# A WKV recurrence on one core: the first group's state steps moved ahead of later pairs, 65 fewer zero matmuls, and constants made later

## The chip, the core and the metric

The kernel runs on one core of a Trainium2 chip. The core has a matrix engine (PE, TensorE; its weight loads are listed as PEld), three engines for elementwise work (DVE, or VectorE; ACT, or ScalarE; POOL, or GpSimd) and SP, which here only issues DMAs. Every engine runs its own list of instructions in the order of the program, and waits on semaphores for the others. ACT and POOL issue DMAs too, each in the order of its own list. 16 DMA engines move the data between HBM and the on-chip memory SBUF; PE writes its results to PSUM, from where DVE and ACT read them.

The metric is the time of one launch in microseconds (us); lower is better.

## The reference

For 16 sequences of 2048 steps and 256 channels, a weighted sum with a decay `w` runs along the sequence, kept stable by a running maximum `pp`:

```
for t in range(seq_len):
    ww = u + kk                      # this step's own weight
    qq = np.maximum(pp, ww); e1 = np.exp(pp - qq); e2 = np.exp(ww - qq)
    output[b, t, :] = (e1 * aa + e2 * vv) / (e1 * bb + e2 + 1e-08)
    ww = pp - w + kk                 # state for the next step
    qq = np.maximum(ww, kk); e1 = np.exp(ww - qq); e2 = np.exp(kk - qq)
    aa = e1 * aa + e2 * vv; bb = e1 * bb + e2; pp = qq
```

Inputs are `k` and `v` (float32, 33.6 MB each), `w` and `u` (256 values each). The output has the shape of `v`.

## The kernel before, in words

**Tiling.** The sequence is cut into 16 groups of 128 steps, and each group into four "pairs" of 4 sequences: 64 pairs, n = 0 to 63, group c = n // 4. A pair is a tile of 128 time steps x 1024 (4 sequences x 256 channels), 0.524 MB of k and as much of v. Inside a pair the recurrence is a sum, done by PE with triangular matrices. Between groups a small state is carried.

**The steps of a pair**, with the names that the code gives them:

- LK, LV load k and v. RK rounds k for PE (DVE or POOL; pairs 3 to 10 do without, as their DMA rounds). CV casts v to bf16 (DVE for n < 10, then POOL).
- R q n and L q n (q = 0, 1): PE puts a row term and the triangular sum of k into one of two PSUM buffers X. X q n: ACT takes the exponential of it into EZR, which frees the buffer.
- TV: DVE multiplies by v. S: PE adds up the pair's totals into TOT.
- DEN, LN, INV: PE forms the denominator in an X buffer, ACT takes Ln and then Exp of the negative. NUM, MUL: PE forms the numerator, DVE multiplies. ST and SQ store the result; SQ is the last quarter of the store, from POOL, for some pairs near the end. They run some ten pairs behind the front (`LAG = 10`).

**The steps of a group**, after its fourth pair's S: CS (copy the totals), TU (PE turns them), SL (ACT, logarithms), FR and OF (DVE, frames and offsets), SW (ACT, weights), CH (DVE, the chain), SS (DVE, spread), TK (PE turns the result back), BK (DVE copies it to `cb`), and SN, KP, which hand the state to the next group. DEN and NUM of a group need its BK.

**The order** is written by a small planner at the end of the function. Each step has a place, a number near its pair's (tables `P`); steps are taken in order of place, as soon as what they come after has been issued and a buffer is free. `AT` overrides a place by name. The order that results is fixed in the program for each engine, which then only waits on semaphores.

**Zeros.** `zeros(m)` issues m matmuls of a zero tile into the PSUM tile TURN; they compute nothing that is used. 26 come at the start; then the planner puts `P["Z0"]` of them ahead of a step of pair 0 or group 0, and `P["Z"]` ahead of others. Between TK and BK, which use TURN, none is issued (`quiet`).

**Setup.** Before the planner runs, DVE clears WUf (a tile for the rows u and w), makes masks and constants, and sets the start values of the state tiles (U, G, TB, CB); POOL shapes the masks. `make_matrices` (step "mats", L182) and the start values (L230 to L236) stand on DVE ahead of the first RK.

In the profile L149 is a zero matmul, L201 R, L207 L, L210 X, L214 CV, L219 TV, L245 S, L251 CS, L258 TU, L262 SL, L267 and L269 FR, L273 to L275 OF, L281 SW, L285 and L288 CH, L295 SS, L302 TK, L306 BK, L322 DEN (into X) and NUM (into num), L330 LN, L338 INV, L350 MUL, L356 and L363 the stores, L194 RK, L108 and L111 LK, L115 LV, and L480 the end of the program.

Of the kernel before, what the change touches and what calls it, by code (L numbers as in the profile page):

```python
# [7 lines left out]
F32 = mybir.dt.float32  # L8
# [3 lines left out]
ACT = mybir.ActivationFunctionType  # L12
# [3 lines left out]
def kernel(  # L16
# [9 lines left out]
    K = tc.keep_in_program_order  # L26
    PE, DVE, SC, POOL, SP = nc.tensor, nc.vector, nc.scalar, nc.gpsimd, nc.sync
# [5 lines left out]
    D = 2 * Dm  # L33
    NP = 4 * NST
# [10 lines left out]
    RS = 2.0 ** -20  # L45
    CAP = 54.0
    BIG = 1e30
# [11 lines left out]
         "R": [-0.795, -7.965],  # L59
         "OUT": {"DEN": [-0.47, -0.155, -0.55, -0.495], "LN": [-11.935, -9.86, -0.84, -6.17], "INV": [-13.87, -8.32, -4.99, -5.82], "NUM": [-0.105, 0.155, 0.11, -5.15], "MUL": [1.115, 0.345, 0.895, 1.035], "ST": [-5.05, 7.26, 1.245, 7.765], "SQ": [-3.365, 6.69, -2.4, 8.84]},  # L60
         "TAIL": {"DEN": -4.36, "LN": -16.54, "INV": 3.8, "NUM": -0.31, "MUL": 4.39, "ST": 14.35, "step": 2.989, "SQ": 26.08},
         "Z0": {"L": 1, "S": 3, "DEN": 0, "NUM": 6, "TK": 47, "TU": 17, "R": 12},
         "Z": {"DEN": 0, "L": 1, "NUM": 0, "TK": 4, "S": 0, "TU": 1, "R": 0}}

    AT = {}

    consts = ctx.enter_context(tc.tile_pool(name="consts", bufs=1))
    kpool = ctx.enter_context(tc.tile_pool(name="kpool", bufs=NK))
# [3 lines left out]
    rpool = ctx.enter_context(tc.tile_pool(name="rpool", bufs=NRD))  # L72
# [14 lines left out]
    def matrix(name, dt):  # L87
        return consts.tile([128, 128], dt, tag=name, name=name)
# [10 lines left out]
    def how(n):  # L99
        return "D" if n < BYSP else FIRST[n] if n < len(FIRST) else PLAN[n % len(PLAN)]  # L100
# [4 lines left out]
    def load_k(n):  # L105
        if how(n) != "C":
            KR[n] = raw(opool, "ot") if n < BYSP else raw(kppool, "kf")
            K((SP if n < BYSP else POOL).dma_start(out=KR[n], in_=rows_of(k, n)))  # L108
        else:
            KR[n] = kpool.tile([128, 4, Dm], F32R, tag="kr", name="kr")  # L110
            K(POOL.dma_start(out=KR[n], in_=rows_of(k, n)))  # L111
# [6 lines left out]
    WUf = rpool.tile([128, 2, D], F32, tag="rd", name="WUf")[:, 0, 0:Dm]  # L118
# [2 lines left out]
    def row_wu(queue, x, g):  # L121
        K(queue.dma_start(out=WUf[g::32, :], in_=bass.AP(tensor=x.tensor, offset=x.offset, ap=[[0, 4], list(x.ap[0])])))

    K(DVE.memset(WUf, 0.0))
    load_k(0)
    row_wu(POOL, u, 1)
    row_wu(SC, w, 0)
# [50 lines left out]
    mats = {name: matrix(name, BF16) for name in ("Id", "IdN", "S", "SN")}  # L178
# [11 lines left out]
    X = [psx.tile([128, 2, D], F32, tag=f"X{a}", name=f"X{a}") for a in range(2)]  # L190
# [31 lines left out]
    AS, D1, L1, A0, FR, BC, A2 = range(7)  # L222
    U_of = [consts.tile([128, 7, 32, 3], F32, tag=f"U{j}", name=f"U{j}") for j in range(2)]
    G_of = [consts.tile([128, 3, 32, 3], F32, tag=f"G{j}", name=f"G{j}") for j in range(2)]
    TB_of = [consts.tile([128, 2, 32, 3], F32, tag=f"TB{j}", name=f"TB{j}") for j in range(2)]
    CB_of = [consts.tile([128, 4, 128], BF16, tag=f"CB{j}", name=f"CB{j}") for j in range(2)]
    AB = consts.tile([128, 2, 32, 3], F32, tag="AB", name="AB")
    st = {}

    for j in range(2):  # L230
        K(DVE.memset(CB_of[j].bitcast(F32), 0.0))
        K(DVE.memset(U_of[j][:, FR, :, 0:1], -BIG))
        K(DVE.memset(G_of[j][:, :, :, 0:1], 0.0))
    K(DVE.memset(U_of[0][:, D1, :, 0:1], -100.0))
    K(DVE.memset(U_of[0][:, L1, :, 0:1], 0.0))
    K(DVE.memset(TB_of[0][:, :, :, 0:1], 0.0))  # L236

    def sums(n):
        c, p = divmod(n, 4)
# [70 lines left out]
    RD, NUM, OT = {}, {}, {}  # L310
# [14 lines left out]
    def den(n, a):  # L325
        apply(X[a], n, ("S", "Id"), 1)

    def log_den(n, a):
        rd = rpool.tile([128, 2, D], F32, tag="rd", name="rd")
        K(SC.activation(rd, X[a], ACT.Ln, scale=RS))  # L330
        RD[n] = rd

    def parts(n):
        return (slice(0, 1), slice(1, 2)) if n == NP - 1 else (slice(0, 2),)

    def inverse(n):
        for i in parts(n):
            K(SC.activation(RD[n][:, i], RD[n][:, i], ACT.Exp, scale=-1.0))  # L338

    def by_x(n):  # L340
        return n >= NP - XT and n % 2 == 1
# [11 lines left out]
    def piece(n, h, queue):  # L353
        c, p = divmod(n, 4)
        t0 = c * TC + HS * (1 - h)
        K(queue.dma_start(out=out[4 * p + 2:4 * p + 4, t0:t0 + HS, :].rearrange("n t d -> t n d"), in_=OT[n][HS * h:HS * h + HS, 2:4, :]))  # L356

    def shared(n):
        return n >= BYPOOL or BYQ[n % len(BYQ)] == "P" and n >= BYF
# [5 lines left out]
            piece(n, h, SP)  # L365

    def store_rest(n):
        piece(n, 1, POOL)


    ops, free = {}, {"K": NK, "KP": NKP, "V": NV, "N": 1, "RD": NRD, "OT": NOT, "VB": NVB}
# [1 line left out]
    def step(name, place, fn, args=(), after=(), take=None, give=(), mode=0):  # L373
        key = name if isinstance(name, str) else " ".join(map(str, name))
        ops[name] = dict(place=AT.get(key, place), fn=fn, args=args, after=list(after), take=take, give=give, mode=mode)

    for n in range(NP):
        c, j = divmod(n, 4)
        early = n < BYSP
        vb = "OT" if n < VOT else "V"  # L380
        put = lambda key: n + P[key][j]
        lead = SOON * max(0.0, 1 - n / UNTIL)
        lag = LAG - sum(n < x for x in LAGS)
        m = n + lag - lead
        tail = n >= NP - LAG
        place = lambda key: m + (P["TAIL"][key] + (n - NP + LAG) * P["TAIL"]["step"] if tail else P["OUT"][key][int(n + lag + 2) % 4])
        kb = "OT" if early else "KP" if how(n) != "C" else "K"
        if n:
            step(("LK", n), n + P["LK"], load_k, (n,), [("LK", n - 1)], kb)
        else:  # L390
            free["OT"] -= 1
        step(("LV", n), n + P["LV"], load_v, (n,), [("LV", n - 1)] + ([("LK", n)] if n else []), vb)
        if how(n) != "C":
            step(("RK", n), put("RK"), round_k, (n,), [("LK", n), ("RK", n - 1)], "K", [kb])
        for q in range(2):
            step(("R", q, n), n + P["R"][q], rows, (n, q), ["wu", ("R", 1 - q, n - 1 + q)], "X", mode=3)
            step(("L", q, n), n + P["L"][q], logs, (n, q), [("R", q, n), ("LK", n), ("RK", n), ("L", 1 - q, n - 1 + q)], None,
                 ["K"] if q else [], 1)
            step(("X", q, n), n + P["X"][q], exps, (n, q), [("L", q, n), ("NUM", n - RING), ("S", n - RING)], None, ["X"])
        step(("CV", n), put("CV"), cast_v, (n,), [("LV", n), ("CV", n - 1)], "VB", [vb])  # L400
        step(("TV", n), put("TV"), times_v, (n,), [("X", 1, n), ("CV", n), ("TV", n - 1)], None, ["VB"])
        step(("S", n), put("S"), sums, (n,), [("TV", n), ("S", n - 1)] + ([("CS", c - 1)] if j == 0 else []), mode=2)
        if j == 3:
            s = P["STATE"][0 if c == 0 else 2 if c == NST - 1 else 1]
            for i, (name, fn, *after) in enumerate((
                    ("CS", copy_sums, ("S", n)), ("TU", turn, ("CS", c), ("CH", c - 1)), ("SL", state_logs, ("TU", c)),
                    ("FR", state_frames, ("SL", c), ("SN", c - 1)), ("OF", state_offsets, ("FR", c)),
                    ("SW", state_weights, ("OF", c)), ("CH", state_chain, ("SW", c), ("KP", c - 1)),
                    ("SS", state_spread, ("CH", c)), ("TK", turn_back, ("SS", c), "mats"), ("BK", copy_back, ("TK", c)),
                    ("SN", state_next, ("OF", c)), ("KP", state_keep, ("CH", c)))):  # L410
                if not (name in ("SN", "KP") and c + 1 == NST):
                    step((name, c), n + s[i] - lead * SHARE, fn, (c,), after, mode=1)
        step(("DEN", n), place("DEN"), den, (n,), [("BK", c), ("DEN", n - 1), "mats"], "X", mode=3)
        step(("LN", n), place("LN"), log_den, (n,), [("DEN", n), ("INV", n - 1)], "RD", ["X"])
        step(("INV", n), place("INV"), inverse, (n,), [("LN", n)])
        step(("NUM", n), place("NUM"), num, (n,), [("BK", c), ("TV", n), ("NUM", n - 1), "mats"], "X" if by_x(n) else "N", mode=3)
        step(("MUL", n), place("MUL"), mult, (n,), [("NUM", n), ("INV", n), ("MUL", n - 1)], "OT", ["X" if by_x(n) else "N", "RD"])
        step(("ST", n), place("ST"), store, (n,), [("MUL", n), ("ST", n - 1)], None, [] if shared(n) else ["OT"])
        if shared(n):
            step(("SQ", n), place("SQ"), store_rest, (n,), [("ST", n)], None, ["OT"])  # L420
    step("mats", P["mats"], make_matrices)
    step("wu", P["wu"], make_rows)

    quiet = False
# [60 lines left out]
```

## Time and profile before

| | us |
|---|---|
| median of 3 runs (lowest to highest) | 292.04 (290.93 to 292.12) |
| the profiled execution | 291.05 |
| its span, first to last instruction | 289.3 |
| busy in the span: PE, ACT, DVE, POOL | 272.0, 258.1, 246.1, 176.9 |

The mean clock granted to PE over the span is 0.988 of full speed. HBM is read for 67.12 MB and written for 33.55 MB.

How to read it. The page shows one execution: the busy time of each engine, the span in 40 slices of 7.2 us (a digit is the busy share in tenths, GB/s is what DMA moved), and groups of instructions. A row of the timeline has the start, the length in us, engine, line, operation, out<-in, shapes and count, and in brackets how long the engine had been idle before and who ended that. A row of sums by stretch has the stretch, its length, then busy time and instruction count of each engine, the granted clock, the DMA share and GB/s. A row of waits has who waited for whom, total us, times, longest. A row of one line's instructions has the count and the shortest, median and longest length in ns, then the first and last start. A `q` behind an engine's name is its sequencer, which issues DMAs and waits. A busy PE is not a PE at its peak, since matmuls are pipelined and their ends are modelled.

### The profile page before, as it was taken

The numbers are of one execution on the slowest core, as the hardware profiler recorded it, in microseconds if no ns is written. First come the engines' busy times: TensorE is split into PE (matmuls) and PEld (weight loads), VectorE is DVE, ScalarE is ACT, GpSimd is POOL, SyncE is SP. The second block draws the span as 40 slices with busy tenths as digits, with TensorE's granted clock in tenths as the row PEclk, the third lists the DMA queues.
The fourth block names the chain that finished last, engine by engine and source line by source line (L and its number), as shares of the span: only waits on it lengthen the run. The fifth ranks groups of instructions, "written<-read, shape, count | busy, mean of one in ns | idle before, by whom it ended". The sixth has DMA issues, their size and how long they took to land.

```text
span 289.3 us, 8057 instructions
## 1 busy us (share of the span) xinstructions
PE 272.0 (94%) x3263; PEld 139.5 (48%) x3263; DVE 246.1 (85%) x423; ACT 258.1 (89%) x290; POOL 176.9 (61%) x219
## 2 busy tenths in 40 slices
PE   7899999999999999999999999999999999997750
PEld 6445744444545455444545454554545455444330
DVE  6666889989898989899897979899898989797860
ACT  1587399999999999999999999999999999997890
POOL 7267367675767686675757686775757674422230
PEclk9999999999999999999999999999999999999995
DMA  7999999999999999999999999999999999896895
GB/s 229 351 347 347 348 343 337 382 328 392 386 393 380 371 387 377 393 383 392 391 381 382 385 385 388 392 365 397 391 391 382 389 363 390 294 247 180 221 265 147
DMA packets 58574, 101.21 MB, mean 350 GB/s; under 512 B 5152, under 2 KB 43560, under 8 KB 58536
## 3 DMA queue, kind: packets, MB, share of 16 engines
q0 software_dynamic: 21248, 65.55, 65.2%
q1 hardware_dynamic: 37280, 35.14, 36.3%
q8 instruction: 25, 0.41, 0.6%
q14 instruction: 13, 0.11, 0.1%
q10 hardware_dynamic: 8, 0.00, 0.0%
HBM read 67.12 MB, written 33.55 MB: 348 GB/s over the span
## 4 chain that ended last, share of the span: by engine, by line
PE 83%; DVE 4%; ACT 4%; issue 3%; POOL 1%; DMA 1%; POOLq 0%; SPq 0%; DVEq 0%
PE X L207 21%; PE X L322 15%; PE num L322 13%; PE X L201 12%; PE TURN L149 12%; PE TOT L245 7%; ACT EZR L210 2%; PE TOT L258 2%; DVE ot L350 1%; PE TURN L302 1%; POOL out_dram L356 1%; DMA out_dram<-ot 1%; ACT rd L330 1%; DVE EZR L219 1%; ACT rd L338 1%
## 5 line engine op out<-in xcount | busy, mean ns | idle before, releaser
L210 ACT ACTIVATE EZR<-X 128x1024 bf16<-128x1024 f32 x128 | 126.8, 1013 | 14.2 <-PE X L207 14.1
L214 POOL CAST vb<-vr 128x1024 bf16<-128x1024 f32 x54 | 56.3, 1042 | 69.7 <-DVE EZR L219 68.1
L219 DVE TENSOR_TENSOR EZR<-EZR,vb 128x2048 bf16<-128x2048 bf16 x64 | 77.8, 1218 | 0.4 <-ACT EZR L210 0.2
L350 DVE TENSOR_TENSOR ot<-num,rd 128x1024 f32<-128x1024 f32 x60 | 73.2, 1220 | 4.6 <-ACT rd L338 3.2
L338 ACT ACTIVATE rd<-rd 128x1024 f32<-128x1024 f32 (+1 forms) x65 | 67.9, 1046 | 2.0
L330 ACT ACTIVATE rd<-X 128x1024 f32<-128x1024 f32 x64 | 65.6, 1025 | 2.5 <-PE X L322 0.9
L149 PE MATMUL TURN<-Z 128*128 128x192 bf16 x319 | 55.7, 261 | 1.6 <-DVE Z L133 1.6
L201 PE MATMUL X<-WU,CO 64*64 64x512 bf16 x512 | 51.9, 390 | 1.1 <-DVE WU L176 0.9
L149 PEld LDWEIGHTS <-Z 128*128 128x128 bf16 x319 | 28.9, 101 | 48.9 <-issue 47.1
L115 POOL DMA_DIRECT2D vr<-in_v_dram x61 | 46.0, 753 | 6.5 <-DVE vb L214 6.5
L207 PE MATMUL X<-kr,NLE 128*128 128x512 f32 x128 | 45.6, 438 | 0.0
L207 PE MATMUL X<-kr,NLZ 128*128 128x512 f32 x128 | 45.5, 437 | 0.0
L108 POOL DMA_DIRECT2D kf<-in_k_dram x53 | 40.2, 758 | 0.0
L194 DVE CAST kr<-kf 128x1024 fp32r<-128x1024 f32 x39 | 30.6, 813 | 4.4 <-DMA kf<-in_k_dram 4.2
L201 PEld LDWEIGHTS <-CO 64*64 64x64 bf16 x512 | 15.7, 105 | 31.4 <-issue 26.4
L322 PE MATMUL X<-EZR,S 64*64 64x512 bf16 x256 | 26.2, 394 | 1.7 <-ACT rd L330 1.0
L322 PE MATMUL X<-cb,Id 64*64 64x512 bf16 x256 | 25.8, 376 | 0.0
L322 PE MATMUL X<-EZR,Id 64*64 64x512 bf16 x256 | 25.8, 376 | 0.0
L322 PE MATMUL num<-EZR,SN 64*64 64x512 bf16 x240 | 24.3, 386 | 1.1 <-DVE ot L350 1.1
L322 PE MATMUL num<-cb,IdN 64*64 64x512 bf16 x240 | 24.0, 376 | 0.0
L322 PE MATMUL num<-EZR,IdN 64*64 64x512 bf16 x240 | 23.9, 376 | 0.0
L245 PE MATMUL TOT<-EZR,OH 128*32 128x256 bf16 x512 | 23.4, 277 | 0.5 <-DVE EZR L219 0.5
(69 smaller groups left out, 270.0 us busy)
## 6 DMA issues: line engine op xcount, KB each, us to landing
vr<-in_v_dram POOLq DMA_DIRECT2D x61, 512.0 KB, 7.9
kf<-in_k_dram POOLq DMA_DIRECT2D x53, 512.0 KB, 8.8
out_dram<-ot SPq DMA_DIRECT2D x64, 256.0 KB, 10.2
out_dram<-ot SPq DMA_DIRECT2D x116, 128.0 KB, 10.1
kr<-in_k_dram POOLq DMA_DIRECT2D x8, 512.0 KB, 8.2
ot<-in_k_dram SPq DMA_DIRECT2D x3, 512.0 KB, 5.0
ot<-in_v_dram SPq DMA_DIRECT2D x3, 512.0 KB, 8.3
out_dram<-ot POOLq DMA_DIRECT2D x12, 128.0 KB, 3.3
```

The source lines that it names most:

```text
L115: K((SP if n < BYSP else POOL).dma_start(out=vr, in_=rows_of(v, n)))
L149: K(PE.matmul(TURN[:, 0:192], Z[:, 0:128], Z, start=first, stop=True, skip_group_check=True))
L201: K(PE.matmul(X[a][o:o + HS, i, :].rearrange("p (n d) -> p n d", n=2), CO[r:r + HS, q, :], WU[r:r + HS, :].unsqueeze(1).broadcast_to([HS, ...
L207: K(PE.matmul(X[a][:, i, :], (NLE, NLZ)[q], km[:, i, :], start=False, stop=True, skip_group_check=True))
L210: K(SC.activation(ez(n)[:, q, 1], X[a], ACT.Exp))
L214: K((DVE if n < EARLY else POOL).tensor_copy(vb, VR.pop(n)))
L219: K(DVE.tensor_mul(ez(n)[:, :, 0], ez(n)[:, :, 1], vb.unsqueeze(1).broadcast_to([128, 2, 2, D])))
L245: K(PE.matmul(t[32 * j:32 * j + 32, 0:256], OH[:, s:s + 32], ez(n)[:, 0, 1 - q, i, 256 * x:256 * x + 256], start=p == 0 and x == 0, stop=p ...
L322: K(PE.matmul(out_tile[o:o + HS, i, :], left, right, start=s == 0, stop=s == 2, tile_position=(r, o), skip_group_check=True))
L330: K(SC.activation(rd, X[a], ACT.Ln, scale=RS))
L338: K(SC.activation(RD[n][:, i], RD[n][:, i], ACT.Exp, scale=-1.0))
L350: K(DVE.tensor_mul(o.rearrange("p (i n) d -> p i (n d)", i=2)[:, i], NUM[n][:, i], RD[n][:, i]))
```

## The change

- **Zeros of pair 0 and group 0**: ahead of each R of pair 0 six instead of 12, ahead of TU 0 none instead of 17, ahead of TK 0 four instead of 47.
- **Places**: `AT` names some twenty steps. TU 0 to SW 0, TV 5, CV 6 and S 4 now stand ahead of pair 7's R; TV 6, CH 0 and SS 0 ahead of pair 8's; S 5, the four zeros, TK 0, BK 0 and S 6 between the two exponentials of pair 8; KP 0 moves behind pair 9, and CV 9 ahead of TV 8. BK 0 stood behind SL 1 before.
- **Quiet stretch**: with TK 0 and BK 0 next to each other, the single zeros ahead of L of pairs 8, 9 and 10 and of TU 1 are issued, seven in all. On PE 65 zeros fewer remain.
- **Constants**: `mats` and the start values (now a step "zero", `start_states`) come behind CV 1 on DVE instead of ahead of RK 0. WUf is cleared by POOL instead of DVE.
- **The last pair**: LN 63 is split in halves like INV 63, each half's Exp behind its Ln; its last quarter's store is issued by ACT instead of POOL.

The order of loads on SP and on POOL is the same in both, as is the order of all steps from RK 11 on, but for the last pair.

```diff
-         "Z0": {"L": 1, "S": 3, "DEN": 0, "NUM": 6, "TK": 47, "TU": 17, "R": 12},
+         "Z0": {"L": 1, "S": 3, "DEN": 0, "NUM": 6, "TK": 4, "TU": 0, "R": 6},
-    AT = {}
+    AT = {"TU 0": 5.01, "FR 0": 5.02, "SW 0": 6.2, "TK 0": 7.205, "CV 7": 6.4, "TV 5": 5.1, "S 4": 5.3, "S 5": 7.195, "TV 6": 6.3, "S 6": 7.21, "S 7": 8.1, "CH 0": 6.32, "SS 0": 6.33, "BK 0": 7.21, "CV 6": 5.2, "TV 7": 7.3, "KP 0": 8.6, "TV 8": 8, "R 0 6": 5.0, "R 0 8": 7.19, "R 0 9": 7.9}
...
-    K(DVE.memset(WUf, 0.0))
+    K(POOL.memset(WUf, 0.0))
...
-    for j in range(2):
-        K(DVE.memset(CB_of[j].bitcast(F32), 0.0))
...
+    def start_states():
+        for j in range(2):
+            K(DVE.memset(CB_of[j].bitcast(F32), 0.0))
...
+    def log_den(n, a):
+        RD[n] = rpool.tile([128, 2, D], F32, tag="rd", name="rd")
+        for i in parts(n):
+            K(SC.activation(RD[n][:, i], X[a][:, i], ACT.Ln, scale=RS))
+            if i.stop == 1:
+                invert(n, i)
+
+    def invert(n, i):
+        K(SC.activation(RD[n][:, i], RD[n][:, i], ACT.Exp, scale=-1.0))
+
     def inverse(n):
-        for i in parts(n):
-            K(SC.activation(RD[n][:, i], RD[n][:, i], ACT.Exp, scale=-1.0))
+        invert(n, parts(n)[-1])
...
-        piece(n, 1, POOL)
+        piece(n, 1, POOL if n < NP - 1 else SC)
...
-... ("SL", state_logs, ("TU", c)),
+... ("SL", state_logs, ("TU", c), "zero"),
...
-    step("mats", P["mats"], make_matrices)
+    step("mats", 1.0, make_matrices)
+    step("zero", 1.01, start_states)
```

More of the change, by code (lines that the diff above doesn't have):

```diff
@@ L228 @@
     st = {}
-    for j in range(2):
[L231 to L236, printed above, removed]
+    def start_states():
+        for j in range(2):
+            K(DVE.memset(CB_of[j].bitcast(F32), 0.0))
+            K(DVE.memset(U_of[j][:, FR, :, 0:1], -BIG))
+            K(DVE.memset(G_of[j][:, :, :, 0:1], 0.0))
+        K(DVE.memset(U_of[0][:, D1, :, 0:1], -100.0))
+        K(DVE.memset(U_of[0][:, L1, :, 0:1], 0.0))
+        K(DVE.memset(TB_of[0][:, :, :, 0:1], 0.0))
     def sums(n):
@@ L326, in den @@
         apply(X[a], n, ("S", "Id"), 1)
[L328 to L331, printed above, removed]
     def parts(n):
         return (slice(0, 1), slice(1, 2)) if n == NP - 1 else (slice(0, 2),)
+    def log_den(n, a):
[6 more added lines that the diff above has]
+        K(SC.activation(RD[n][:, i], RD[n][:, i], ACT.Exp, scale=-1.0))
     def inverse(n):
-        for i in parts(n):
-            K(SC.activation(RD[n][:, i], RD[n][:, i], ACT.Exp, scale=-1.0))
+        invert(n, parts(n)[-1])
     def by_x(n):
@@ L405 @@
             for i, (name, fn, *after) in enumerate((
-                    ("CS", copy_sums, ("S", n)), ("TU", turn, ("CS", c), ("CH", c - 1)), ("SL", state_logs, ("TU", c)),
+                    ("CS", copy_sums, ("S", n)), ("TU", turn, ("CS", c), ("CH", c - 1)), ("SL", state_logs, ("TU", c), "zero"),
                     ("FR", state_frames, ("SL", c), ("SN", c - 1)), ("OF", state_offsets, ("FR", c)),
```

## The prediction

> **What bounds the kernel now.** I read the page first, for who is busy; then sums by stretch, for how the start differs from the middle; then the timeline from 16 to 50 us, where every moved step lies; last the timeline of the end.
>
> ```profile
> PE 272.0 (94%) x3263; PEld 139.5 (48%) x3263; DVE 246.1 (85%) x423; ACT 258.1 (89%) x290; POOL 176.9 (61%) x219
> ACT  1587399999999999999999999999999999997890
> GB/s 229 351 347 347 348 343 337 382 328 392 386 393 380 371 387 377 393 383 392 391 381 382 385 385 388 392 365 397 391 391 382 389 363 390 294 247 180 221 265 147
> 3.00:40.00 37.00, 35.85 (x329) 21.60 (x328) 26.34 (x60) 22.08 (x24) 19.72 (x32) 1.00 1.28 350
> 50.00:250.00 200.00, 199.67 (x2444) 98.15 (x2437) 184.42 (x295) 196.82 (x223) 137.30 (x156) 1.00 1.04 383
> ```
>
> In the two sums the columns are length, busy time of PE, PEld, DVE, ACT and POOL, granted clock, DMA share, GB/s. From 50 to 250 us ACT has work for 196.82 of 200 us; that stretch is ACT's. In the fill, 3 to 40 us, ACT works 22.08 of 37, and PE's 35.85 contain the zero matmuls. The ACT row's "3" is the hole that the change aims at:
>
> ```profile
> 28.98 4.05 PE L149 MATMUL TURN<-Z 128*128 128x192 bf16 x47
> 34.84 2.02 ACT L210 ACTIVATE EZR<-X 128x1024 bf16<-128x1024 f32 x2 [4.38 <-PE X L207]
> ```
>
> ACT idles 4.38 us while PE does 47 zeros, the turn back (TK 0) and two sums ahead of pair 8. That is what one would like to win. But the DMA rate in the fill is flat (350 GB/s over the stretch, 343 to 351 in the second to sixth slice of 7.2 us), hole or no hole, and the consumers of loads tell when loads arrive:
>
> ```profile
> 16.98 0.73 DVE L214 CAST vb<-vr 128x1024 bf16<-128x1024 f32 x1 [0.79 <-DMA vr<-in_v_dram]
> 27.37 0.69 DVE L214 CAST vb<-vr 128x1024 bf16<-128x1024 f32 x1 [1.06 <-DMA vr<-in_v_dram]
> 39.40 1.04 POOL L214 CAST vb<-vr 128x1024 bf16<-128x1024 f32 x1 [1.62 <-DMA vr<-in_v_dram]
> 40.39 1.04 POOL L194 CAST kr<-kf 128x1024 fp32r<-128x1024 f32 x1
> 40.80 1.16 DVE L194 CAST kr<-kf 128x1024 fp32r<-128x1024 f32 x1 [1.16 <-DMA kf<-in_k_dram]
> ```
>
> These are CV 3, CV 6 and CV 10 waiting for v3, v6 and v10, then RK 11 without a wait, and RK 12 waiting for k12. From v6 to v10 are four pairs in 12.03 us, 3.01 us a pair. Two loads of 0.524 MB in 3.01 us are 348 GB/s, the whole rate of the windows. So loads come one each 1.50 us whatever the engines do, and k12, one load behind v10, is met 1.40 after it. The change keeps the order of all loads on SP and POOL, and nothing that it moves lets them start sooner. **These arrivals stay.**
>
> **The change, part by part.**
>
> *Zeros.* Ahead of R 0 0 and R 1 0 six go each, 17 ahead of TU 0, 43 ahead of TK 0: 72 out. TK 0 and BK 0 are now close together, so seven single zeros that lay in the quiet stretch between them come back (two for each of pairs 8, 9, 10, one ahead of TU 1). Net 65; at 4.05/47 = 0.086 us, 5.6 us of PE. What this reaches is decided by the arrivals.
>
> *Head.* WUf's memset goes from DVE to POOL, and the constants and start states (4.59 to 6.22) leave DVE ahead of RK 0.
>
> ```profile
> 0.93 0.27 DVE L124 MEMSET WUf<- 128x256 f32 x1 [0.93 <-PEq L469]
> 1.50 0.75 POOL L122 DMA_DIRECT2D WUf<-in_u_dram  x1 [0.99 <-DVE I L131]
> 4.59 0.27 DVE L231 MEMSET CB<- 128x256 f32 x1
> 6.22 0.68 DVE L194 CAST kr<-ot 128x1024 fp32r<-128x1024 f32 x1
> 7.87 0.41 PE L201 MATMUL X<-WU,CO 64*64 64x512 bf16 x4 [0.88 <-DVE WU L176]
> ```
>
> POOL idles 0.99 ahead of u's DMA, so a memset (about 0.26 at the 1.04 for 1024 elements of its cast above) fits in. The first R gains between 0 (the row u lands no sooner) and 1.6 us (6.22 less 4.59); the six zeros gone ahead of R 1 0 add 0.5. I take 1.0 in all for pairs 0 to 5, and it reaches nothing, as pair 6 meets its arrival. The 1.6 us of constants and states now stand ahead of CV 2 on DVE, which, its own work being 1.0 earlier, makes CV 2 about 0.6 late: hidden by DVE's wait for v3 up to 16.98. Without that cover 0.6 us would sit in front of S 1.
>
> *First group's steps.* TU 0, SL 0, FR 0, OF 0, SW 0 move ahead of pair 7, TK 0 and BK 0 behind pair 8, and TV 5, CV 6, S 4 to S 6 between. PE loses the hole, and then runs into the loads, which are issued k(n+1), v(n): v10 is at 39.3, so k11 at 37.8, v9 at 36.3, k10 at 34.8, and L 0 10 starts at 34.9 at best. On DVE the new order is CV 9 (v9, 36.3), TV 8, CS 1: 36.4 + 0.69 + 1.22 + 0.42 = 38.7. TU 1 then starts at about 38.75.
>
> ```profile
> 40.31 0.58 PE L258 MATMUL TOT<-Sel,ts 128*128 128x96 f32 x4
> 40.82 0.41 PE L322 MATMUL X<-EZR,S 64*64 64x512 bf16 x4
> 41.89 0.21 DVE L267 TENSOR_TENSOR U<-U 128x64 f32<-128x64 f32 x1
> 43.15 1.22 DVE L219 TENSOR_TENSOR EZR<-EZR,vb 128x2048 bf16<-128x2048 bf16 x1
> 43.22 0.71 PE L207 MATMUL X<-kr,NLE 128*128 128x512 f32 x2
> 44.88 0.62 PE L245 MATMUL TOT<-EZR,OH 128*32 128x256 bf16 x16
> 45.43 0.41 PE L322 MATMUL X<-EZR,S 64*64 64x512 bf16 x4
> 46.32 1.02 ACT L330 ACTIVATE rd<-X 128x1024 f32<-128x1024 f32 x1 [0.16 <-PE X L322]
> 49.40 0.41 PE L322 MATMUL X<-EZR,S 64*64 64x512 bf16 x4
> 50.28 1.03 ACT L330 ACTIVATE rd<-X 128x1024 f32<-128x1024 f32 x1
> ```
>
> From TU 1 (40.31) to L 0 11 (43.22) are 2.91 us of PE work: L 0 11 at 41.65, by when RK 11 (40.39 + 1.04 on POOL) is just done. R, L of pair 11 and S 8 take 44.88 - 43.22 = 1.66: PE is at S 9 at 43.3. S 9 needs TV 9, and TV 9 follows RK 12, which starts at 40.80 with k12 in both kernels; from 40.80 to 43.15 DVE is busy without a break, so TV 9 still ends at 44.37. S 9 at 44.4, DEN 1 at 44.77: **0.66 earlier than 45.43**. LN 1 follows (46.32, ACT then runs on). DEN 2 needs X(0,12) done and TK 1 out of the way: 48.85 for 49.40, LN 2 0.55 earlier. Of 5.6 us of zeros and a hole of 4.38, 0.55 is left on ACT.
>
> Does it stay through 200 us? ACT is 98.4% busy there, which speaks for it. Against it: DMA is at 383 GB/s, and DVE still meets loads:
>
> ```profile
> DVE kr L194 <- DMA kf<-in_k_dram: 3.1, 7, 0.6
> ```
>
> Seven times in 200 us (3.1 in all) RK waits for its k, and an earlier ACT only waits there longer, as at 40.80. Bounds: 0 and 0.66. I take 0.4, nearer to ACT's row, since DVE has 15.6 us of slack in that stretch to swallow such waits.
>
> *End.* The last pair's Ln is split in halves, and the last quarter's store (SQ 63) goes from POOL to ACT's queue.
>
> ```profile
> 279.56 1.00 ACT L330 ACTIVATE rd<-X 128x1024 f32<-128x1024 f32 x1
> 280.60 1.15 ACT L338 ACTIVATE rd<-rd 128x512 f32<-128x512 f32 x2
> 281.20 0.61 POOL L356 DMA_DIRECT2D out_dram<-ot  x1 [1.40 <-DVE ot L350]
> 281.36 0.60 SPq L356 DMA_DIRECT2D out_dram<-ot  x1
> 282.70 0.60 SPq L356 DMA_DIRECT2D out_dram<-ot  x1
> 282.84 0.61 POOL L356 DMA_DIRECT2D out_dram<-ot  x1 [1.03 <-DVE ot L350]
> L480 POOLq DRAIN  x3: 46/161/5381, 282.8 to 289.1; - x3
> L480 SPq DRAIN  x3: 7/7/7, 287.2 to 288.7; - x3
> ```
>
> ACT now does Ln, Exp, Ln, Exp on halves: 4 x 0.575 = 2.3 for 2.15 us, and each Exp waits on its own Ln; the last half is 0.15 to 0.3 later. The earlier first half is worth nothing, as SP is issuing pair 62's piece until 281.96. POOL's drain begins with its last store (282.8), lasts 5.38 and ends at 288.2; SP has seen all landings at 287.2. So POOL ends the kernel, 1.0 us after SP. Without that store POOL's drain starts after pair 62's, 1.6 us earlier (281.2 + 5.4 = 286.6), and SP decides: 1.0 gained, less the late half (0.2) and less what a store from ACT costs over SP's 0.60; the one on record took 1.11:
>
> ```profile
> 1.24 1.11 ACTq L122 DMA_DIRECT2D WUf<-in_w_dram  x1
> ```
>
> That is 0 to 0.5. So 0.3 to 0.8 (0 if the drain doesn't hang on the store; a loss of 0.3 if only the split counts); I take 0.6.
>
> The Trainium skill, "DMA: Bandwidth & Descriptors", Specifications, gives a first byte about 0.4 us sooner from a scalar-engine queue than from GpSimd. By it (an estimate) the end would gain 0.4 more; no row here isolates it.
>
> **Sum.** 0.4 + 0.6 = 1.0 off the profiled execution: span 289.3 to 288.3, time 291.05 to 290.05. The median of the three runs is 292.04, 1.0 above it; against that, which is how the changed kernel will be told, 291.0 us.
>
> **Rivals.**
> - *The hole comes back whole.* If loads aren't the pace, ACT wins 4.38 and the time is about 287; if half, 289. For it: before 41 us only the four waits quoted above are put down to loads. Against it: rate and arrivals above, with nothing late on POOL. Chance 0.11.
> - *Nothing arrives.* The load waits take the 0.4 back, and the drain or the ACT store takes the 0.6: 291.6 to 292.2. For it: 383 GB/s. Chance 0.24.
> - *Slower: PE's clock drops.* The zeros keep PE busy. Afterwards PE is idle from L 1 10's end (about 36.5) to TU 1 at 38.75, 2.2 us. A drop to half is in this trace (stretches of 3.41 us; the clock is the third column from the end):
>
> ```profile
> 275.54:278.95 3.41, 2.39 (x44) 1.27 (x40) 2.45 (x2) 3.35 (x5) 0.88 (x2) 1.00 0.93 275
> 278.95:282.37 3.42, 1.16 (x24) 0.46 (x15) 2.34 (x3) 2.76 (x4) 1.21 (x2) 1.00 0.88 250
> 282.37:285.78 3.41, 0.00 (x0) 0.00 (x0) 0.18 (x1) 0.00 (x0) 0.61 (x1) 0.50 0.93 259
> ```
>
> A stretch with PE busy 2.39 kept the clock, one with 1.16 lost it for the next. The new gap leaves 3.41 - 2.2 = 1.2 busy when it falls into one stretch. One stretch at half costs 1.7 us of PE, of which 1.1 is the new idle before TV 9: the 0.66 is gone, 291.4. Two in a row: 3.4 - 1.1 - 0.66 - 0.6 = 1.0 slower, 293.1; from three on (294.8) it is slower beyond the 0.5% that a measurement here can tell from no change. Chance 0.10, of it 0.06 beyond. The Trainium skill, "TensorE: Matmul & The Clock Gate", Why this matters for your kernels, asks for gaps over about 3 us before the clock drops; by that rule 2.2 us costs nothing and the sum stands. The trace disagrees: the clock fell at 282.37, under 2.3 us after the last matmul ended.
>
> **How the numbers follow.** Forecast 0.55 (290.2 to 291.6; 0.22 of it under 290.58, since end and fill may both come at their upper bounds), the others as given. Half a percent of 292.04 is 1.46. Faster: 0.22 + 0.11 = 0.33. Slower: 0.06. Same: 0.61, which is 0.33 of the forecast, 0.24 and 0.04. Range 289.5 to 292.7: it leaves out the whole hole and the clock lost twice; 290.2 to 291.6 is the forecast's own.
>
> **What would show it.** Right: ACT's first Ln of pair 1 about 0.6 before 46.32; RK 12 again at 40.8 on a load; DMA at about 350 GB/s through the fill; PE idle near 37 to 38.7 with clock 1.00; no POOL drain past 287; the last DMA issue on ACT's queue. Wrong: RK 12 well before 40.5, a clock under 1 before 280, or ACT busy no earlier at 50 us.

## The result, and the profile after

The changed kernel takes 290.69 us (median of 20 runs, 290.12 to 292.61), the kernel before beside it on the same chip 291.68 (20 runs, 290.93 to 292.29): a ratio of 0.9975, 95% interval 0.9964 to 0.9986. One microsecond is won, within half a percent. The profiled execution took 290.14 us with a span of 288.4.

First the page of the changed kernel: busy time of the engines, ACT's busy tenths and the DMA rate in 40 slices of 7.2 us.

```profile
PE 269.3 (93%) x3198; PEld 134.7 (47%) x3198; DVE 246.5 (85%) x422; ACT 258.5 (90%) x291; POOL 176.3 (61%) x219
...
ACT  1787658999999999999999999999999999997891
...
GB/s 218 350 351 345 351 345 325 388 345 390 381 388 360 377 392 377 396 378 395 383 386 383 387 389 374 391 370 395 384 396 390 379 385 357 327 258 172 228 257 189
```

PE has the 65 matmuls fewer that were counted (3198 for 3263). ACT's row no longer has a "3": the hole of the fill is shared out over its slices. The rate of the fill is what it was. The sums by stretch of the changed kernel: the fill, the middle, and the stretches of 3.41 us around 40 us.

```profile
3.00:40.00 37.00, 32.97 (x279) 17.19 (x277) 26.40 (x60) 23.75 (x26) 19.27 (x32) 1.00 1.29 350
50.00:250.00 200.00, 199.27 (x2440) 97.93 (x2437) 184.96 (x295) 196.70 (x223) 136.98 (x156) 1.00 1.04 381
36.90:40.32 3.42, 1.70 (x20) 1.10 (x21) 1.67 (x3) 1.03 (x3) 0.87 (x1) 1.00 1.04 352
40.32:43.73 3.41, 3.41 (x24) 1.28 (x21) 2.77 (x8) 1.89 (x2) 3.41 (x5) 0.50 1.08 321
43.73:47.15 3.42, 3.42 (x54) 1.61 (x53) 3.31 (x8) 3.06 (x4) 2.76 (x5) 1.00 0.95 333
```

ACT does 23.75 us of work before 40 us for 22.08, so the hole did give something to ACT. Then PE, busy for 1.70 of 3.42 us, gets half its clock for the next 3.41. The timeline of the changed kernel shows what stood there, and what came of it:

```profile
36.40 0.69 DVE L214 CAST vb<-vr 128x1024 bf16<-128x1024 f32 x1 [2.30 <-DMA vr<-in_v_dram]
...
38.62 0.69 PE L259 MATMUL TOT<-Sel,ts 128*128 128x96 f32 x4 [2.14 <-DVE ts L252]
...
39.45 1.04 POOL L214 CAST vb<-vr 128x1024 bf16<-128x1024 f32 x1 [4.30 <-DMA vr<-in_v_dram]
...
40.85 1.17 DVE L194 CAST kr<-kf 128x1024 fp32r<-128x1024 f32 x1 [2.29 <-DMA kf<-in_k_dram]
...
42.73 1.17 PE L207 MATMUL X<-kr,NLE 128*128 128x512 f32 x2
43.20 1.22 DVE L219 TENSOR_TENSOR EZR<-EZR,vb 128x2048 bf16<-128x2048 bf16 x1
...
45.40 0.41 PE L323 MATMUL X<-EZR,S 64*64 64x512 bf16 x4
...
46.29 1.03 ACT L335 ACTIVATE rd<-X 128x1024 f32<-128x1024 f32 x1 [0.16 <-PE X L323]
```

These are CV 9 on v9, TU 1, CV 10 on v10, RK 12 on k12, L 0 11, TV 9, DEN 1 and LN 1. The loads are met at the same times as before (39.45 for 39.40, 40.85 for 40.80); only the waits for them are longer, 4.30 for 1.62 and 2.29 for 1.16. At the end of it LN 1 stands at 46.29 for 46.32: in this execution the fill gave 0.03 us.

Later, the waits of the stretch from 50 to 250 us of the changed kernel, and the timeline and the last instructions of its end:

```profile
DVE kr L194 <- DMA kf<-in_k_dram: 3.6, 8, 0.8
PE num L323 <- DVE ot L355: 0.4, 1, 0.4
```

```profile
279.87 0.58 ACT L335 ACTIVATE rd<-X 128x512 f32<-128x512 f32 x1
...
283.02 0.74 ACTq L361 DMA_DIRECT2D out_dram<-ot  x1
283.02 0.60 SPq L361 DMA_DIRECT2D out_dram<-ot  x1
```

```profile
L486 POOLq DRAIN  x3: 46/93/5102, 281.5 to 288.1; - x3
L486 SPq DRAIN  x3: 7/7/7, 287.3 to 287.6; - x3
```

RK waits for its k once more than before (eight times for seven), PE once for a MUL (0.4, which the kernel before does not show), and the last pair's Ln starts 0.31 late (279.87 for 279.56). This is not the fill's: the run with the store alone, below, has the fill of the kernel before, and the same wait and the same start. The end then takes 8.5 us from there (288.4 - 279.87) where it took 9.7 (289.3 - 279.56). POOL's drain starts at 281.5 and lasts 5.10, so it ends at 286.6, and SP closes the kernel at 287.3. The whole gain of this execution is the end's.

### The profile page after: what moved, and what is told of

Read it like the earlier page. It is cut to its first block, busy times and chain, and to the rows that moved or that the text cites. A ratio compares the mean times of both kernels' runs of the same rounds, so it can differ in the third digit from the quotient of the medians.

```text
span 288.4 us, 7927 instructions
## 1 busy us (share of the span) xinstructions
PE 269.3 (93%) x3198; PEld 134.7 (47%) x3198; DVE 246.5 (85%) x422; ACT 258.5 (90%) x291; POOL 176.3 (61%) x219
## 4 chain that ended last, share of the span: by engine, by line
PE 74%; ACT 7%; DMA 6%; DVE 4%; issue 3%; POOL 2%; SPq 0%; POOLq 0%; DVEq 0%
PE X L207 18%; PE X L323 15%; PE num L323 13%; PE X L201 10%; PE TURN L149 9%; PE TOT L246 6%; DMA vr<-in_v_dram 4%; ACT rd L335 3%; ACT EZR L210 3%; PE TOT L259 2%; DVE ot L355 2%; ACT rd L340 2%; DMA WUf<-in_u_dram 2%; DVE EZR L219 1%; PE TURN L303 1%
## 5 line engine op out<-in xcount | busy, mean ns | idle before, releaser
L335 ACT ACTIVATE rd<-X 128x1024 f32<-128x1024 f32 (+1 forms) x65 | 65.8, 1012 | 3.1 <-PE X L323 1.5
L149 PE MATMUL TURN<-Z 128*128 128x192 bf16 x254 | 51.9, 268 | 1.5 <-DVE Z L133 1.4
L149 PEld LDWEIGHTS <-Z 128*128 128x128 bf16 x254 | 24.0, 103 | 50.4 <-issue 48.8
L194 DVE CAST kr<-kf 128x1024 fp32r<-128x1024 f32 x39 | 31.4, 834 | 5.9 <-DMA kf<-in_k_dram 5.9
```

The costliest lines, as they stand in the source:

```text
L149: K(PE.matmul(TURN[:, 0:192], Z[:, 0:128], Z, start=first, stop=True, skip_group_check=True))
L335: K(SC.activation(RD[n][:, i], X[a][:, i], ACT.Ln, scale=RS))
```

## The experiments

Each median stands beside that of the kernel before, run in turn with it on the same chip. "Theory A" is the prediction's own: loads pace the fill.

**The end's two edits in the kernel before.** The first run has both, the second the store alone.

```diff
-        piece(n, 1, POOL)
+        piece(n, 1, POOL if n < NP - 1 else SC)
# the first run also: the Ln of the last pair in halves, as in the change
```

> The kernel before with only the last pair changed: its last quarter's store from ACT's queue, and its Ln in halves. Theory A (the gain is the end's, since loads hold the fill back and a clock drop took the rest): 1.0 to 1.3 us faster, ratio about 0.996. Theory B (the moved steps and the missing zeros of the fill give the gain): no change, within 0.2 us. Either way POOL's long drain ends before SP has seen the last landing.

> The kernel before with only the last quarter's store moved from POOL to ACT; Ln in one piece. Theory A, with the store as the whole of the end's gain: 1.0 to 1.4 us faster, the same as with the split or 0.1 better, as the split puts 0.15 more on ACT. If the split is what pays, 0.5 us or less. Theory B: no change.

290.78 us and 290.77, for 291.77: ratios 0.9966 (0.9952 to 0.998) and 0.9968 (0.9956 to 0.9981). So the end is worth 1.0, all of it the store's, and the split nothing. Of the run with the store alone, a wait from 50 to 250 us, the last pair's Ln, and the last instructions:

```profile
PE num L322 <- DVE ot L350: 0.4, 1, 0.4
...
279.87 1.00 ACT L330 ACTIVATE rd<-X 128x1024 f32<-128x1024 f32 x1
...
L480 POOLq DRAIN  x3: 51/102/5308, 281.5 to 288.3; - x3
L480 SPq DRAIN  x3: 7/7/7, 287.5 to 287.8; - x3
```

POOL's drain starts with pair 62's store and is over at 286.8, ahead of SP, as in the changed kernel. The wait of 0.4 and the Ln at 279.87 are those of the changed kernel too.

**The fill alone**: the changed kernel without the end's two edits.

```diff
-        piece(n, 1, POOL if n < NP - 1 else SC)
+        piece(n, 1, POOL)
# and the Ln of the last pair whole again
```

> The changed kernel with the old end: all moves, zeros and constants of the fill, but one Ln and the last store from POOL. Theory A: within 0.4 us of before, to either side, and RK 12 again waits for its load at about 40.8 us. Theory B: about 1.0 us faster, ratio about 0.9965.

291.72 us for 291.77, ratio 0.9998 (0.9984 to 1.0011): the fill is worth nothing that can be measured. Its sums by stretch:

```profile
36.97:40.38 3.41, 1.16 (x16) 0.78 (x16) 2.16 (x3) 0.95 (x2) 0.34 (x1) 1.00 1.03 348
40.38:43.80 3.42, 3.42 (x32) 1.39 (x24) 2.24 (x8) 2.08 (x2) 3.42 (x5) 0.50 0.92 299
```

The half clock is here too. Whether it took the gain, or there was none, the next run tells apart.

**24 zeros in PE's gap**, ahead of TU 1, where the changed kernel has one.

```diff
+    WARM = 24
-            zeros(P["Z0" if name[-1] < FILL else "Z"].get(name[0], 0))
+            zeros(WARM if name == ("TU", 1) else P["Z0" if name[-1] < FILL else "Z"].get(name[0], 0))
```

> The changed kernel with 24 zeros instead of one ahead of the second group's turn (TU 1), in the 2.1 us for which PE waits there. Theory A: the granted clock stays 1.00 through the fill, the Ln of pair 1 starts about 0.6 us before the 46.3 of the changed kernel's profile, and the time is 0 to 0.6 us below the changed kernel's, with a smaller spread. If only the clock, not the loads, held the fill back: that Ln starts 2 us or more earlier. If the clock drop did not matter: no difference to the changed kernel.

290.03 us for 291.77, ratio 0.9941 (0.9923 to 0.9959). Its timeline, and the stretch with the former gap:

```profile
38.58 0.69 PE L260 MATMUL TOT<-Sel,ts 128*128 128x96 f32 x4 [0.15 <-DVE ts L253]
...
41.59 0.71 PE L208 MATMUL X<-kr,NLE 128*128 128x512 f32 x2
...
44.60 0.41 PE L324 MATMUL X<-EZR,S 64*64 64x512 bf16 x4
...
45.49 1.02 ACT L336 ACTIVATE rd<-X 128x1024 f32<-128x1024 f32 x1 [0.96 <-PE X L324]
```

```profile
35.45:38.87 3.42, 3.27 (x33) 2.54 (x30) 2.16 (x3) 2.04 (x2) 0.00 (x0) 1.00 1.02 347
38.87:42.28 3.41, 3.41 (x45) 1.67 (x44) 1.59 (x3) 2.37 (x3) 3.02 (x4) 1.00 1.02 347
```

TU 1 starts no later than without the zeros (38.58 for 38.62), the clock stays whole, and L 0 11, DEN 1 and LN 1 come at 41.59, 44.60 and 45.49: the times that the prediction had worked out, 0.8 ahead of the kernel before at LN 1. The time is about 0.7 us below the changed kernel's, a little more than the 0.6 expected at most, and the executions lie closer together (289.47 to 290.93). Work that does nothing makes this kernel faster.

**Are the loads the pace?** The kernel before and the changed one, both with eight loads of v left out ("light" from here on). The edit is the same in both:

```diff
+    ONE = consts.tile([128, 4], F32, tag="ONE", name="ONE")
+    K(DVE.memset(ONE, 1.0))
     def load_v(n):
+        if 4 <= n < 12:
+            VR[n] = ONE.unsqueeze(2).broadcast_to([128, 4, Dm])
+            return
```

> The kernel before with the loads of v of pairs 4 to 11 left out: their cast reads a resident column of ones instead, so those pairs' output is not the reference's; every engine's instructions stay, only eight 0.5 MB transfers (8 x 1.50 us = 12 us of the fill's transfers) go. Theory A (arrivals set the pace of the fill): the kernel before has PE full in every window of the fill with its 76 zeros, so it can win little: 0 to 1.5 us below the kernel before. This run is the partner of the next one.

> The changed kernel with the same eight loads left out (those pairs' output is not the reference's). Theory A (arrivals, not PE, set the fill, so 65 zeros fewer bought nothing): with the arrivals out of the way the 5.6 us of PE work can become time: 2 to 4 us below the light kernel before, 1.0 of it the end's. Theory B (the zeros never lay on the path, whatever the loads do: the first group's chain of ACT and DVE steps or the matmuls' own order holds the fill): the difference stays at the end's 1.0 us.

290.64 us and 285.88 (the kernel before, whole: 291.62). LN 1 in the timeline of the light kernel before, and of the light changed one:

```profile
46.37 1.03 ACT L335 ACTIVATE rd<-X 128x1024 f32<-128x1024 f32 x1 [0.16 <-PE X L327]
```

```profile
42.29 1.02 ACT L340 ACTIVATE rd<-X 128x1024 f32<-128x1024 f32 x1 [0.16 <-PE X L328]
```

With the loads out of the way the same edit is worth 4.08 us at LN 1 and 4.76 in the time; theory B falls, and the gain is even larger than the 2 to 4 us that theory A expected. Most casts of v take 0.69 us on DVE in both light kernels, as with the loads, so it is not the cast that became cheaper. The light kernel before stands where the whole one did (46.37 for 46.32): there PE and its zeros were a second pace, no faster than the loads. Its time is 1.0 us below the whole one's, within the 0 to 1.5 expected, but not from the fill, as LN 1 shows; in its trace it comes in the end (see the last section).

**The zeros alone** in the kernel before, **and the moves alone** (the changed kernel with the old zeros).

```diff
# zeros alone, in the kernel before:
-... "TK": 47, "TU": 17, "R": 12},
+... "TK": 4, "TU": 0, "R": 6},
# moves alone: the same two lines the other way round, in the changed kernel
```

> The kernel before with the three counts of zeros alone (4, 0 and 6 for 47, 17 and 12), nothing moved. Theory A: arrivals pace the fill, so 65 zeros fewer give 0 to 0.4 us: 291.2 to 291.8. Rival (the zeros are on the path and it is the moves that give their 5.6 us back): 2 us or more faster, 289.8 or less.

> The changed kernel with the old counts of zeros (47, 17 and 12 for 4, 0 and 6): the moved places, the late start states and the end alone. The end gives 1.0 us, as in the two runs of the end. Theory A (arrivals pace the fill; the zeros only keep PE busy in the meantime): no stretch of PE under 60% busy and so no half clock, but 47 zeros (4 us) now stand ahead of the moved carries, whose followers were placed for 4; the fill is 0 to 1 us longer than before: 290.6 to 291.8. Rival (the moves themselves shorten the fill, whatever the zeros): 290.2 or less.

The zeros alone: 292.69 us for 291.62, ratio 1.0034 (1.0013 to 1.0055, reckoned without the longest execution, 295.47). That is slower, which neither side had expected. Its sums by stretch name a cause:

```profile
29.48:32.90 3.42, 1.29 (x24) 0.67 (x24) 2.95 (x7) 0.34 (x1) 0.58 (x1) 1.00 1.46 350
32.90:36.31 3.41, 3.41 (x16) 1.27 (x16) 3.20 (x5) 1.10 (x2) 1.49 (x2) 0.50 1.06 347
```

With TK 0 where it was, PE stands waiting for the chain of the first group (3.09 us ahead of TK 0) instead of doing zeros, and pays with the clock. The mean granted clock that is on record for each execution fits: 0.967 to 0.987 in these twelve, 0.988 to 0.993 in the kernel before beside them. The moves alone: 291.33 us for 291.55, ratio 0.9982 (0.9969 to 0.9996); less the end's 1.0, the fill has become 0.8 longer, as theory A had it. Neither half of the fill's edit gains anything alone.

**The heads of two queues.** The changed kernel, with CS 1 and TV 8 ahead of CV 9 on DVE and RK 11 ahead of CV 10 on POOL; and, in a second kernel, TV 9 ahead of RK 12 on DVE as well.

```diff
-... "TV 8": 8, ...
+... "TV 8": 8.15, "CS 1": 8.11, "CV 9": 8.3, "RK 11": 9.19, ...
# the second kernel also: "TV 9": 9.0, "CV 11": 10.75
```

> The changed kernel with four places more: the second group's copy of sums and the times-v of pair 8 go ahead of the cast of v 9 on DVE, and the rounding of k 11 ahead of the cast of v 10 on POOL. Theory A in its narrow form (two instructions that wait for a load, v 9 at 36.3 us and v 10 at 39.4 us, stand at the head of an engine's queue with work behind them that is ready): the turn of the second group leaves 38.62 us for about 34.9, the first denominator moves from 39.24 to about 37.6, the logs of pair 11 from 42.73 to about 41, and the time falls by 1.0 to 1.9 us against the changed kernel, to 288.8 to 289.7. Rival (the sum of the arrivals paces the fill, whatever the order on the engines): 0 to 0.3 us below the changed kernel.

> The kernel with the four places more, and two more: the times-v of pair 9 ahead of the rounding of k 12 on DVE (it waited 3.22 us behind that wait for a load), the cast of v 11 kept where it was. Theory A (a wait for a load at the head of an engine's queue is what is left in the fill, and a PE under 60% busy in one stretch of 3.41 us is what halves its clock in the next): the sums of pair 9 leave 44.19 us for about 42.6, PE's 1.63 us of idle time ahead of them go, no half clock in the fill in any execution, 0.5 to 1.1 us below the undisturbed executions of the run with four places (289.2 to 289.9), so 288.5 to 289.2. Rival (arrivals of k 12 and v 11 hold what comes behind anyway): 289.2 to 289.9, but without the executions at 291.4 to 292.6 if the clock's part is right.

The first: 290.04 us for 291.62, ratio 0.9963 (0.994 to 0.9985), eight of its twelve executions at 289.2 to 290.42 and four at 291.44 to 292.63. The mean granted clock on record is 0.983 to 0.985 in these four and 0.989 to 0.995 in the eight. The profiled one is of the four. Its timeline and stretches:

```profile
38.00 0.41 PE L323 MATMUL X<-EZR,S 64*64 64x512 bf16 x4
...
40.93 0.82 DVE L194 CAST kr<-kf 128x1024 fp32r<-128x1024 f32 x1 [3.22 <-DMA kf<-in_k_dram]
...
42.92 1.22 DVE L219 TENSOR_TENSOR EZR<-EZR,vb 128x2048 bf16<-128x2048 bf16 x1
...
44.19 0.40 PE L246 MATMUL TOT<-EZR,OH 128*32 128x256 bf16 x6 [1.63 <-DVE EZR L219]
```

```profile
41.24:44.65 3.41, 1.78 (x27) 0.79 (x27) 3.31 (x9) 2.21 (x3) 2.01 (x4) 1.00 1.02 346
44.65:48.06 3.41, 3.41 (x30) 1.48 (x26) 3.00 (x7) 2.06 (x2) 3.41 (x5) 0.50 1.03 348
```

TU 1 started at 35.01 for 38.62 in the changed kernel, and DEN 0 came 1.2 us earlier (38.00 for 39.24), nearly as the narrow theory said. But RK 12 met k12 at 40.93 (40.85 in the changed kernel), TV 9 and S 9 waited behind it, and the gap on PE had only moved, with the half clock behind it. The time, 0.6 us below the changed kernel's, lies between the two forecasts and bears out neither.

The second kernel missed its forecast: 291.48 us for 291.55, ratio 0.9995 (0.9973 to 1.0017). In its timeline:

```profile
41.39 0.82 DVE L194 CAST kr<-kf 128x1024 fp32r<-128x1024 f32 x1 [2.29 <-DMA kf<-in_k_dram]
...
43.02 1.37 DVE L275 TENSOR_TENSOR U<-U 128x64 f32<-128x64 f32 x1
...
43.24 1.05 POOL L214 CAST vb<-vr 128x1024 bf16<-128x1024 f32 x1
...
44.52 1.21 DVE L355 TENSOR_TENSOR ot<-num,rd 128x1024 f32<-128x1024 f32 x1
...
45.78 0.64 PE L323 MATMUL num<-EZR,SN 64*64 64x512 bf16 x4 [2.29 <-DVE ot L355]
```

S 9 no longer waits, but MUL 0 (44.52) still stands behind RK 12 on DVE, which in this execution met k12 at 41.39; NUM 1 waits for MUL 0, and the gap on PE is 2.29 us instead of 1.63, again with half the clock in the next stretch. About half of that gap has another cause: TV 9's early end had set CV 11 free to run on POOL at 43.24, amid the second group's frames, where one small DVE instruction ahead of MUL 0 took 1.37 us for its usual 0.23. The rival was right that arrivals hold what comes behind; its time, and its second half (no executions above 291.4), fell with the theory's. Here too the time goes with the clock on record: seven executions of 291.26 to 292.92 us have 0.983 to 0.986, five of 289.96 to 290.65 us have 0.990 to 0.993.

**18 zeros in the gap of the first of these two**, ahead of S 9.

```diff
+    WARM = 18
-            zeros(P["Z0" if name[-1] < FILL else "Z"].get(name[0], 0))
+            zeros(WARM if name == ("S", 9) else P["Z0" if name[-1] < FILL else "Z"].get(name[0], 0))
```

> The kernel with the four places more, and 18 zeros (1.6 us) on PE ahead of the sums of pair 9, where it stood idle for 1.63 us (42.56 to 44.19). Theory A (the executions of that kernel at 291.4 to 292.6 are those in which a stretch of 3.41 us ends with PE busy less than about 60% of it, so that the next goes at half clock): the slow executions go, all lie at 289.2 to 290.4, median about 289.5. Rival (the spread has another cause, such as later waits for loads): still a third of the executions over 291, median 290 as before.

289.8 us for 291.43, ratio 0.9945 (0.9927 to 0.9963), all six executions at 289.2 to 290.55. None lies at 291.4 or above, where a third of the twelve had been, and none has a mean clock under 0.988; six are few, but the gap was what differed. LN 1 in its timeline:

```profile
45.36 1.02 ACT L336 ACTIVATE rd<-X 128x1024 f32<-128x1024 f32 x1 [1.21 <-PE X L324]
```

That is 0.13 ahead of the kernel with the 24 zeros and the old order (45.49). So in these two traces the order at the heads of the queues is worth 0.13. The arrival of k12 bounds both: TV 9 follows RK 12 on DVE without a break (40.92 to 42.86 here, 40.65 to 43.00 there).

**The best version**: the 24 zeros, with the last pair's Ln whole.

```diff
# the kernel with WARM = 24, and log_den and inverse as in the kernel before
```

> The changed kernel with 24 zeros for 1 ahead of the second group's turn (as in the run with 24 zeros) and the last pair's log whole again. Theory A (the split is worth nothing, the 24 zeros keep the clock): 289.7 to 290.3, as the run with 24 zeros had 290.03. Rival (the split is worth the 0.2 us that I gave it): 0.2 or more slower than that run, 290.2 to 290.5.

289.68 us for 291.55, ratio 0.9936 (0.9921 to 0.995). It beats both kernels, and without the split nothing is lost: the rival's 290.2 to 290.5 did not come.

## Why the prediction came out

The time, 290.69 us for a forecast of 291.0, is within the forecast's own range. That the gain of 1.0 us came out so exactly is in part luck: of its two terms the fill was put too high by about as much (0.35) as the end was put too low (0.4).

- *Arrivals stay*: right. v10 and k12 were met within 0.05 us of before, and the pair of light kernels shows that the loads, not PE, keep the 65 zeros from becoming time.
- *The head reaches nothing, the steps up to DEN 1*: right as a mechanism. The first R came 0.76 us earlier (7.11 for 7.87); no run has the head alone, but the steps behind it came where the forecast had them without it. Forecast TU 1 38.75, L 0 11 41.65, DEN 1 44.77; with the clock kept they came at 38.58, 41.59 and 44.60. In the changed kernel itself TU 1 came at 38.62, and the later steps late.
- *Fill 0.4*: mis-sized; 0.05 measured, not told from nothing. The failing step is what followed from PE's idle 2.14 us: the forecast kept the clock at 1.00 behind it and gave the drop to a rival, with a chance of 0.10. In the profiled executions of the changed kernel and of its fill alone the drop is there (one of the signs that the forecast had named as wrong), and its price is the rival's: 1.7 us of PE less the idle time took the 0.66, LN 1 at 46.29 for 45.66 forecast.
- *How often the clock drops*: the mean granted clock on record for each execution tells it. One stretch at half clock takes 0.006 off it (half of 3.41 us in 288.4); the rest that it lacks to 1 is lost at the end, where PE has no more work. The 19 executions of the two runs of the end lie at 0.990 to 0.995; of the changed kernel's 20, thirteen lie at 0.977 to 0.989, eight of them at 0.987 or below. So the drop came in about half of the executions or more. It is not the whole account: the other seven, at 0.990 and above, took 290.34 to 291.10 us, median 290.58, which is 1.1 below the kernel before's 291.68, little more than the end's 1.0. What else the 24 zeros mend, if it is not chance among few executions, stays open.
- *Does it stay through 200 us?* In the traces it does. With the clock kept, in the kernel with 24 zeros, LN 2 is 0.71 earlier than in the kernel before (49.57 for 50.28) and the last pair's Ln 0.68 earlier than in the run with the store alone (279.19 for 279.87), which has the same wait of 0.4 on the way. The time is 0.75 below the run of the end's two edits (290.03 for 290.78). The load waits that spoke against it are there, but did not take the gain back.
- *End 0.6*: mis-sized, 1.0 measured. The gap between POOL and SP, 1.0, was read rightly; the two deductions, 0.2 for the late half and 0.2 for the store on ACT, came to nothing together. The ACT queue took 0.74 for that store, not the 1.11 of the start, and ran beside SP's. SP's drain starts 7.4 us after the last pair's Ln (279.87 to 287.3), where it was 7.6 (279.56 to 287.2).
- *"TensorE: Matmul & The Clock Gate"* of the Trainium skill, Why this matters for your kernels, warns of PE idle gaps over about 3 us. The runs disagree: a gap of 2.14 us was enough in the changed kernel, and one of 1.63 us in the kernel with four more places.

## What to carry to other kernels

Before removing idle work from an engine, look whether it is the only one that is late: where two paces lie side by side, taking one away moves the waits to the other (the same edit was worth 4 us without eight of the loads, and nothing with them). Filler on PE can be worth keeping, as long as it ends before the work that PE waits for. At the end of a kernel look which queue closes it, and take the last transfer off that queue.

## What was not expected of the hardware

- **A gap of under 2 us on PE can cost half the clock, and PE's busy share does not say when.** Stretches of 3.41 us in the fill in which PE was busy 1.16, 1.29, 1.70 and 1.78 us were followed by one at half clock; the forecast's stretch with 2.39 was not, nor were those of 3.27 and more. Yet at the end of the run with the store alone a stretch with 1.49 kept the clock for the next one:

```profile
278.64:282.06 3.42, 1.49 (x24) 0.71 (x23) 2.30 (x3) 3.35 (x5) 1.15 (x2) 1.00 0.92 262
282.06:285.47 3.41, 0.00 (x0) 0.00 (x0) 0.80 (x2) 0.00 (x0) 0.06 (x1) 1.00 0.89 263
```

So no bound on the busy time of a stretch fits all of these, the 60% of three expectations included (PE's busy time is itself modelled), and what the clock goes by stays open. The edges of the stretches lie differently in each trace (one at 36.90 in the changed kernel, at 35.45 in the one with 24 zeros), which may be why the same kernel keeps its clock in some executions and not in others; with one trace of each kernel that is not shown.
- **A cast on POOL can hold a small DVE instruction for a microsecond**: 1.37 us for 0.23, ending 0.09 after a POOL cast of 1.05. Two other traces have the like: 0.85 and 0.86 us for 0.23 beside a POOL cast of k of 1.50, in the light changed kernel (37.55) and in the run of the moves alone (42.91), each ending 0.07 after the cast. The Trainium skill, "SBUF — State Buffer", SBUF: two separate sides, has the two engines share a port pair, which the one that starts first holds for its whole instruction while the other is blocked. The lengths agree with it. The order in the first case does not, as far as the records go: there DVE's instruction starts 0.23 us before the cast.
- **The light kernel before ends sooner.** It has the same last stores as the whole one, yet ends 8.9 us after the last pair's Ln (279.60 to 288.5) instead of 9.7. Its last instructions:

```profile
L485 POOLq DRAIN  x3: 51/93/4827, 282.9 to 288.2; - x3
```

POOL's drain took 4.83 us for 5.38, with eight loads fewer issued by POOL in all. That the loads are why is not shown: in the traces with all loads this drain lasts from 4.71 us (the second kernel of the two with moved heads) to 5.76 (the moves alone).
